# A two-layer hybrid backbone on one core: context rows turned four experts at a time, the last expert's rows added on chip, recurrent products regrouped

## The chip, the cores and the metric

The kernel is one program on one core of a Trainium2 chip. The engines that the rows name are TensorE (PE: products, and transposes that are products with an identity; PEld is its weight load), VectorE (DVE), ScalarE (ACT), GpSimd (POOL) and SyncE (SP, whose queue issues most transfers). The metric is device microseconds of one execution, less is better. The kernel before took 3310.74 us as the median of three runs (3307.70 to 3312.14).

## The reference

Two layers work on 1024 latent tokens of width 1024 beside 256 context tokens. Every layer is a mixer, a residual, and a mixture of 16 experts, and each part is preceded by RMSNorm with a gain, a shift and a scale from a conditioning vector:

```python
# layer 0, chunkwise, both directions (GLA; the SSD half is alike)
att = where(tril, (q*exp(b-b_ref)) @ (k*exp(b_ref-b)).T, 0)        # 64x64 per chunk and head
o   = att @ v + (q*exp(b)) @ S ;  S' = exp(b_last)*S + (k*exp(b_last-b)).T @ v
# layer 1: latent attention, 8 heads of 128, over context and latent keys
o   = softmax(scale*(qn@kn.T + qr@kr.T)) @ v ;  x += m2 * (o @ w_o)
# both layers: each of 16 experts chooses its tokens (cap = 2*T/16)
aff = softmax(h @ w_router) ; g, idx = top_k(aff.T, cap)
hid = silu(h[idx] @ w_gate) * (h[idx] @ w_up)
x[idx] += m5 * g * (hid @ w_down)
```

An expert takes 128 latent rows, and in layer 0 also 32 context rows; layer 1 has no context rows in its mixture. All is float32 outside; the large products run as three products of high and low parts (`mm3`, L135 to L140: high x high L138, high x low L139, low x high L140), and the parts come from `split` (L142 to L145: high part on ScalarE L144, low part on VectorE L145).

## The kernel before

The stages follow each other in time: the recurrent mixer of layer 0 (0 to 883 us), its tail with out-projection, router and choice of tokens (to 1076), the first mixture (to 1887), the latents of layer 1 (to 2010), attention (to 2510), the second tail (to 2681), the second mixture (to 3281), and the end. In the mixers, tails, latents and attention the order of TensorE's work is written out by hand: generators yield an estimate in microseconds of what they have issued, and others are let on by it. In the two mixtures a scheduler orders every engine from the order in which the code issues.

Recurrent mixer. `gla_chain` (L709) works on two heads of ten blocks of 128 tokens, four chains in all. `scores` (L754) makes the masked score tile `am` of a block, on TensorE (L768) and VectorE (L773, L774). The loop at L805 multiplies it with `v` (L820, one product a head) and adds the states' share, up to four 64x64 products a head (L823). For chains 0 and 1 the scores of the next block are issued ahead of a block's products, for chains 2 and 3 behind them; `cov` (L111 and on) holds the side work in microseconds that is issued at each yield.

Tails. `tail` (L1427) runs `mixed` (L1373): tile by tile the out-projection with `wo`, and, one tile late, `router` (L892) and `affinities` (L915). `choose` (L951) searches the thresholds of the 16 experts and leaves `ch_slot` (L1053). In the second tail the eight raw tiles `owr` of `w_o` are loaded by SP (L847) into tiles that share their place with the residual's (tags `rx`, `rxm`, `rh`, `m2`, `m4`, `m3`) and split into two 32 KB tiles `wo`. `router` loads its three row blocks `rg` (L897), transposes them (L899) and folds them into the router's weights.

First mixture. `experts` (L1152), lower half. A `pick` (L1164) makes the row numbers of one expert (`route`, L1069: `rt_hot` by comparison L1073, products L1075, `rt_i` L1079), and GpSimd gathers 128 rows `xg` (L1161); for expert 0 it also runs `top_context` (L1084), which finds the context rows of all experts, and it gathers 32 context rows `xgc`. `prep` turns `xg` (8 transposes of 128x128, L1195) and `xgc` (8 of 32x128, L1203). `gate_up` multiplies per half of the hidden width two chunks of gate and up by `mm3`, and the context rows by the raw chunks in 32 small products (`mm_context`, L1143). `activate` (L1250) makes `sil` for the latent rows and `hc` for the context rows, `turn` (L1262) transposes `sil` (L1266) and `hc` (4 of 32 rows, L1272). `down` (L1276) does four chunks; behind the second and the fourth it multiplies the context rows in 16 small products. `add_rows` (L1296) scales (`ye`, L1297) and scatters with an add (L1298). A raw chunk of 1 MB comes over SP (L1124) into one of eight places (five of a ring and three spare); the low parts of the first two chunks are made by GpSimd in eight pieces (L1132). For the last expert, eight conditioning products (`mod_round`, L296) follow the last product, and then the latents begin: `load` (L1540) reads the first pair of x tiles behind the last scatter, `norm` squares (L1551) and scales (L1555) them, `turn` transposes (L1562). The splits of the latents' weights `wd` precede `norm` in the code.

Second mixture. Only latent rows; `wide_gate_up` (L1217) and `down` of the expert before, as a pipeline: down(e-1) is issued behind gate and up of e, and the turn of e's `sil` (L1266) behind the second and fourth chunk of down(e-1).

## Time and profile before

| what | value |
|---|---|
| median of the runs | 3310.74 us (3307.70 to 3312.14) |
| profiled execution, its own time | 3311.28 us |
| its span, first to last instruction | 3309.5 us |
| mean granted TensorE clock | 0.962 of full speed |
| TensorE busy | 3051.5 us, 92% of the span |
| VectorE, ScalarE, GpSimd busy | 2264.7, 1683.3, 683.7 us |
| moved by DMA | 624.92 MB, mean 189 GB/s |

The page of the profile gives the span in 40 slices of 82.7 us; TensorE's clock, in tenths:

```profile
PEclk8999999999799899999999999999998979999999
```

Busy time is that of instructions on the engine; time that an engine spends waiting is not busy, and the timeline puts it in brackets ahead of the row that ended it, with what released it. A duration of a product in the timeline is longer than its distance to the next one, as products are pipelined: the distance from start to start is what one costs in a dense stretch.

### The profile page before, as it was taken

The numbers are of one execution on the slowest core, as the hardware profiler recorded it, in microseconds if no ns is written. First come the engines' busy times: TensorE is split into PE (matmuls) and PEld (weight loads), VectorE is DVE, ScalarE is ACT, GpSimd is POOL, SyncE is SP. The second block draws the span as 40 slices with busy tenths as digits, with TensorE's granted clock in tenths as the row PEclk, the third lists the DMA queues.
The fourth block names the chain that finished last, engine by engine and source line by source line (L and its number), as shares of the span: only waits on it lengthen the run. The fifth ranks groups of instructions, "written<-read, shape, count | busy, mean of one in ns | idle before, by whom it ended". The sixth has DMA issues, their size and how long they took to land.

```text
span 3309.5 us, 50386 instructions
## 1 busy us (share of the span) xinstructions
PE 3051.5 (92%) x19910; PEld 2382.1 (72%) x19910; DVE 2264.7 (68%) x3526; ACT 1683.3 (51%) x2405; POOL 683.7 (21%) x730
## 2 busy tenths in 40 slices
PE   5999989897897899999999899999998879999997
PEld 4878776686675566666666587888886658887775
DVE  4774463535657777777777676666665588988887
ACT  4444342635221556556566444555553247766675
POOL 3134461426211312212212110000000100111111
PEclk8999999999799899999999999999998979999999
DMA  6112144234764687887887712100106569999995
GB/s 212 47 31 63 41 133 154 57 90 151 243 211 133 235 292 266 286 296 263 286 295 266 253 55 49 30 23 22 26 9 229 188 235 379 373 358 368 367 358 183
DMA packets 252798, 624.92 MB, mean 189 GB/s; under 512 B 47876, under 2 KB 107482, under 8 KB 222866
## 3 DMA queue, kind: packets, MB, share of 16 engines
q1 hardware_dynamic: 227154, 545.17, 45.5%
q0 software_dynamic: 25408, 76.54, 8.3%
q8 instruction: 156, 2.56, 0.3%
q14 instruction: 80, 0.66, 0.1%
HBM read 560.71 MB, written 60.92 MB: 188 GB/s over the span
## 4 chain that ended last, share of the span: by engine, by line
PE 35%; issue 20%; DVE 5%; POOL 4%; ACT 3%; DMA 2%; SPq 0%; POOLq 0%; ACTq 0%; DVEq 0%
PE acc L139 7%; PE acc L140 7%; PE acc L138 7%; PE tp L138 2%; PE tp L139 2%; PE tp L140 2%; PE tp L1788 2%; POOL xl L1298 1%; POOL xc L1298 1%; DMA xl<-ye,rt_i 1%; POOL xg L1161 1%; PE s L1757 1%; PE s L138 1%; PE s L140 1%; PE s L139 1%
## 5 line engine op out<-in xcount | busy, mean ns | idle before, releaser
L145 DVE TENSOR_TENSOR wcl<-wc,wch 128x2048 fp32r<-128x2048 f32 x380 | 874.3, 2308 | 208.0 <-ACT wch L144 206.9
L144 ACT ACTIVATE wch<-wc 128x2048 fp32r<-128x2048 f32 x380 | 728.0, 1918 | 360.5 <-PE acc L140 317.3
L139 PE MATMUL acc<-wcl,xt 128*128 128x512 f32 x1024 | 408.5, 399 | 0.3 <-DVE wcl L145 0.3
L138 PE MATMUL acc<-wch,xt 128*128 128x512 f32 x1024 | 405.9, 404 | 1.8 <-ACT xt L144 1.8
L140 PE MATMUL acc<-wch,xt 128*128 128x512 f32 x1024 | 406.8, 398 | 0.0
L138 PEld LDWEIGHTS acc<-wch,xt 128*128 128x128 f32 x1024 | 194.5, 190 | 72.5 <-issue 25.1
L140 PEld LDWEIGHTS acc<-wch,xt 128*128 128x128 f32 x1024 | 193.9, 189 | 45.4
L139 PEld LDWEIGHTS acc<-wcl,xt 128*128 128x128 f32 x1024 | 194.3, 190 | 43.5 <-DVE wcl L145 0.7
L139 PE MATMUL acc<-wcl,ht 128*128 128x512 f32 x512 | 206.7, 404 | 8.1 <-DVE wcl L145 8.1
L138 PE MATMUL acc<-wch,ht 128*128 128x512 f32 x512 | 209.0, 408 | 0.4 <-ACT wch L144 0.4
L140 PE MATMUL acc<-wch,ht 128*128 128x512 f32 x512 | 202.8, 396 | 0.0
L1298 POOL DMA_INDIRECT xl<-ye,rt_i x31 | 103.1, 3326 | 457.8 <-DVE ye L1297 457.8
L138 PE MATMUL mm<-ahi,w 128*128 128x512 f32 (+1 forms) x480 | 182.6, 380 | 0.0
L139 PE MATMUL mm<-alo,w 128*128 128x512 f32 (+1 forms) x480 | 173.2, 361 | 0.0
L140 PE MATMUL mm<-ahi,w 128*128 128x512 f32 (+1 forms) x480 | 173.1, 361 | 0.0
L1161 POOL DMA_INDIRECT xg<-hl,rt_i x32 | 75.4, 2356 | 400.6 <-issue 176.1
L138 PE MATMUL mm<-w,ahi 128*128 128x256 f32 (+1 forms) x480 | 148.5, 309 | 2.5 <-DVE tm L432 2.5
L144 ACT ACTIVATE pt<-tp 128x512 fp32r<-128x512 f32 (+1 forms) x192 | 98.3, 528 | 101.9 <-PE tp L1788 100.7
L145 DVE TENSOR_TENSOR pt<-tp,pt 128x512 fp32r<-128x512 f32 (+1 forms) x192 | 113.7, 594 | 44.5 <-ACT pt L144 44.3
L140 PE MATMUL mm<-w,alo 128*128 128x256 f32 (+1 forms) x480 | 137.8, 287 | 0.0
L139 PE MATMUL mm<-w,ahi 128*128 128x256 f32 (+1 forms) x480 | 137.7, 287 | 0.0
L138 PE MATMUL acc<-wo,ot 128*128 128x512 f32 x288 | 120.2, 417 | 5.1 <-ACT wo L144 5.1
(530 smaller groups left out, 7090.1 us busy)
## 6 DMA issues: line engine op xcount, KB each, us to landing
wc<-in_w_gate SPq DMA_DIRECT2D x128, 1024.0 KB, 7.4
wc<-in_w_up SPq DMA_DIRECT2D x128, 1024.0 KB, 8.8
wc<-in_w_down SPq DMA_DIRECT2D x128, 1024.0 KB, 8.2
w<-in_w_mod SPq DMA_DIRECT2D x32, 1024.0 KB, 5.3
craw<-in_w_in SPq DMA_DIRECT2D x40, 256.0 KB, 3.1
wm<-in_w_mod SPq DMA_DIRECT2D x8, 1024.0 KB, 10.1
wc<-in_w_mod SPq DMA_DIRECT2D x8, 1024.0 KB, 10.3
xl<-rxm POOLq DMA_DIRECT2D x16, 512.0 KB, 5.5
```

Of the source, the lines that this page charges most:

```text
L138: mm(out, a[0], b[0], start=first, stop=False, skip_group_check=skip)
L139: mm(out, a[0], b[1], start=False, stop=False, skip_group_check=skip)
L140: mm(out, a[1], b[0], start=False, stop=last, skip_group_check=skip)
L144: self.nc.scalar.activation(hi, src, AF.Copy)
L145: self.nc.vector.tensor_sub(lo, src, hi)
L1161: return nc.gpsimd.indirect_dma_start(out=out, out_offset=None, in_=src, in_offset=bass.IndirectOffsetOnAxis(ap=idx, axis=0))
L1298: nc.gpsimd.indirect_dma_start(out=rows[i], out_offset=bass.IndirectOffsetOnAxis(ap=idx, axis=0), in_=y, in_offset=None, compute_op=OP.add)
L1757: nc.tensor.matmul(out, qrl[:, q], krs[:, ks], start=False, stop=True)
L1788: nc.tensor.transpose(p[:, 128 * j:128 * j + 128], pr[:, 128 * (t0 + j):128 * (t0 + j) + 128], self.ident)
```

## The change

Nine edits, in the order of the code:

1. `gla_chain`: in a block first both heads' products with `am`, then the states' products in the order direction, half, head. For chains 0 and 1 the scores of the next block are issued behind the block's products.
2. `router` yields behind its row loads; `mixed` issues the router's weights and the first router's rows at its very start.
3. `mod_round` yields once per chunk of its loop.
4. `affinities` takes a call `amid`; in the first tail's last affinities it makes expert 0's row numbers and issues its gather (`first_rows`).
5. The low parts of the first two chunks of the first mixture go from GpSimd to VectorE, behind the gather.
6. First mixture: context rows of four experts are gathered into one 128-row tile, three experts ahead, and turned by eight full transposes for four experts; `top_context` and the first four gathers are issued between gate and up of the first chunk; both halves of `hc` lie in one 128-row tile and are turned by four full transposes; down's context products of all eight k stand in one group behind the last chunk.
7. Second mixture: the two turns of an expert's `sil` move into the next expert's gate and up (behind chunks 0 and 2).
8. End of the first mixture: the latents' first pair of x tiles is loaded ahead of the last scatter, and the last expert's rows are added to it on chip by products with a 0/1 matrix (`add_last`).
9. Second tail: the eight staging tiles of `w_o` are allocated ahead of `wo`, with the tags in another order, and `wo` consists of 16 tiles of 4 KB a partition.

The core of the diff:

```diff
-    pooled, gated = (2, 0), (0, 2)
+    pooled, gated = (0, 0), (2, 2)
...
-            yield 1.0 / per
+            if k % per == per - 1:
+                yield 1.0
...
+            if not ahead:
+                yield self.cov[4]
+            po = p[:, :, 128:192]
+            for h in range(2):
+                nc.tensor.matmul(po[:, h, :], a[:, h, :], v[:, blk, 64 * h:64 * h + 64], start=True, stop=False,
+                                 skip_group_check=True)
+            ops = [(d, half, h) for d, first in ((0, 0), (1, 3)) for half in range(2) if 2 * blk + half != first
+                   for h in range(2)]
+            for j, (d, half, h) in enumerate(ops):
+                n, ch = 2 * blk + half, slice(64 * h, 64 * h + 64)
+                nc.tensor.matmul(po[64 * half:64 * half + 64, h, :], gates[d][1][ch, 64 * n:64 * n + 64],
+                                 ts[d][ch, n, :], start=False, stop=(j >= len(ops) - 2), skip_group_check=True)
+            nc.scalar.activation(oh[:, blk], po, AF.Copy)
...
-            nc.scalar.activation(oh[:, blk], po, AF.Copy)
+                yield self.cov[4]
...
             nc.sync.dma_start(rows[8 * j:8 * j + 8, :], src.rearrange("(k p) -> k p", p=128))
+        yield None
...
+        if amid:
+            amid()
...
+    def first_rows(self, picked, src, pool):
+
+        nc = self.nc
+        xg = self.ring_chunk(self.ring)[:, :D]
+        fetched = nc.gpsimd.indirect_dma_start(out=xg, out_offset=None, in_=src,
+                                               in_offset=bass.IndirectOffsetOnAxis(ap=picked[0], axis=0))
+        return picked, xg, self.one_behind(fetched, pool)
+
+    def one_behind(self, issue, pool):
+
+        one = pool.tile([128, 1], F32, name="one")
+        with self.tc.issue_after(issue.ins):
+            self.nc.gpsimd.memset(one, 1.0)
+        return one
...
+        def lows(one):
+            for raw, hi, lo in early:
+                nc.vector.scalar_tensor_tensor(lo, raw, one, hi, op0=OP.mult, op1=OP.subtract)
+
...
+            if e == 0 and two:
+                picked[0], xg, one = routes[0][3]
+                lows(one)
+                return xg
+            picked[e] = self.route(e, *routes[0][:2], routes[0][2] if two else pool, tp())
...
+            if early:
+                lows(self.one_behind(fetched, pool))
+            if two and e + 3 < NE:
+                pick_context(e + 3)
+            return xg
+
+        def pick_context(e):
+
+            if e % 4 == 0:
+                four.append(pool.tile([128, D], F32, name="xgc", bufs=1))
+            gather(hs[1], routes[1][0][:, e:e + 1], four[-1][32 * (e % 4):32 * (e % 4) + 32, :])
+
+        def choose_context():
+            routes[1] = self.top_context(routes[1], pool, tp)
+            for c in range(4):
+                pick_context(c)
+
+        def prep_context(xgc):
+            xct = pool.tile([128, KT, 128], F32, name="xct", bufs=1)
+            for half in range(2):
+                p = tp()
+                for j in range(4):
+                    k = 4 * half + j
+                    nc.tensor.transpose(p[:, 128 * j:128 * j + 128], xgc[:, 128 * k:128 * k + 128], self.ident)
+                nc.scalar.activation(xct[:, 4 * half:4 * half + 4, :], p.rearrange("p (k t) -> p k t", t=128), AF.Copy)
+            return xct
...
+                if half == 0 and e % 4 == 0:
+                    turned_rows[0] = prep_context(four.pop(0))
+                xct = turned_rows[0]
...
+                    self.mm_context(cg, xct[:, :, 32 * (e % 4):32 * (e % 4) + 32], [held[2 * (kk // 4) + m][0][:, kk % 4, :] for m in range(2)], kk)
...
+        def both(acc, half=0):
+
+            here, there = slice(64 * half, 64 * half + 64), slice(64 - 64 * half, 128 - 64 * half)
+            sc = pool.tile([128, 512], F32, name="sc", bufs=1)[here]
+            nc.scalar.activation(sc, acc[there, :], AF.Copy)
+            nc.vector.tensor_add(sc, sc, acc[here, :])
...
+            if two:
+                sc = both(cg, half)
+                h = hc[64 * half + 32:64 * half + 64, :]
+                nc.scalar.activation(h, sc[0:32, :], AF.Silu)
+                nc.vector.tensor_mul(h, h, sc[32:64, :])
+            return sil
...
+        def turn_context(hct):
+
+            p = tp()
+            for j in range(4):
+                nc.tensor.transpose(p[:, 128 * j:128 * j + 128], hc[:, 128 * j:128 * j + 128], self.ident)
+            src = p.rearrange("p (k h t) -> p h k t", h=4, t=32)
+            nc.vector.tensor_copy(hct.rearrange("p (h k) t -> p h k t", h=2), src[:, 1::2])
...
-            if two and q % 2:
-                for kk in range(4):
-                    self.mm_context(cy, hct, [held[kk // 2][:, kk % 2, 512 * m:512 * m + 512] for m in range(2)],
-                                    2 * q - 2 + kk)
+            if two and q == 3:
+                with self.tc.issue_after(latest.ins):
+                    for kk in range(KT):
+                        self.mm_context(cy, hct, [held[kk // 2][:, kk % 2, 512 * m:512 * m + 512] for m in range(2)],
+                                        kk)
...
+                        if e and q % 2 == 0:
+                            turn(q // 2, hid[q // 2], late)
...
-                    if e < NE and q % 2:
-                        turn(q // 2, hid[q // 2], ht, None)
+                    if e == NE - 1 and q % 2:
+                        turn(q // 2, hid[q // 2], ht)
...
-            gate_up(e, 0, 0, x, *a0)
+            gate_up(e, 0, 0, x, *a0, choose_context if e == 0 else None)
...
-            turn(1, h1, ht, hct)
+            turn(1, h1, ht)
+            turn_context(hct)
...
+                self.first_x = self.first_tiles(xs[0])
...
+            ye = pool.tile([128, D], F32, name="ye", bufs=1)
+            add_rows(0, idx, gate, ye, ay[0].rearrange("p a f -> p (a f)"))
+            if e == NE - 1:
+                self.add_last(self.first_x, parts, ye.rearrange("p (a f) -> p a f", a=2), pool, psum)
...
+        self.wr = self.router_weights(l, pool)
+        routed = self.router(l, tiles[0][0], pool, psum)
+        next(routed)
...
+                        if n > 1:
+                            routed = self.router(l, late[0], pool, psum)
+                            next(routed)
+                        next(routed)
...
+            if l == 0 and found and not begun:
+                begun.append(self.first_rows(self.route(0, found[0], pay, mc, psum("tp")), self.hd[0], mc))
...
+        begin()
+        routes = [(found[0], pay, mc, *begun)]
...
-        xs = [x_tile() for _ in range(2)]
+        xs = self.first_x
...
-        load(order[0], xs)
...
+
+        xs = [self.first_tile(j) for j in range(2)]
+        for j, x in enumerate(xs):
+            t = 2 * self.order[0] + j - 2
+            self.nc.sync.dma_start(x, src[128 * t:128 * t + 128, :])
+        return xs
+
+    def add_last(self, xs, parts, y, pool, psum):
+
+        nc = self.nc
+        base = 128 * (2 * self.order[0] - 2)
+        tok = pool.tile([128, 256], F32, name="tok_row", tag="xg", bufs=2)
+        nc.gpsimd.iota(tok, pattern=[[1, 256]], base=base, channel_multiplier=0, allow_small_or_imprecise_dtypes=True)
+        at = pool.tile([128, 1], F32, name="tok_at")
+        nc.vector.tensor_add(at, parts[:, 0:1], parts[:, 1:2])
+        hot = pool.tile([128, 256], F32R, name="hot", tag="xg", bufs=2)
+        nc.vector.tensor_scalar(hot, tok, at, None, op0=OP.is_equal)
+        h = [pool.tile([128, 2, 512], F32R, name=f"yh{j}", tag=f"xt{j}", bufs=1) for j in range(2)]
+        self.split(*h, y)
+        for j, x in enumerate(xs):
+            p = psum.tile([128, 2, 512], F32, name="fp", tag="acc", bufs=2)
+            for m in range(2):
+                for i in range(2):
+                    nc.tensor.matmul(p[:, m], hot[:, 128 * j:128 * j + 128], h[i][:, m], start=(i == 0), stop=(i == 1))
+            nc.vector.tensor_add(x, x, p.rearrange("p a f -> p (a f)"))
...
-                    wo = [pool.tile([128, KT, D], F32R, name=f"wo{j}") for j in range(2)]
+                    tags = ("m2", "m4", "m3", "rh", "rx", "rx", "rxm", "rxm")
+                    staged = [pool.tile([128, D], F32, name="owr", tag=t, bufs=2 if "x" in t else 1) for t in tags]
+                    wo = [Rows([pool.tile([128, D], F32R, name=f"wo{j}{k}") for k in range(KT)]) for j in range(2)]
...
-                    tags = ("rx", "rxm", "rx", "rxm", "rh", "m2", "m4", "m3")
-                    stage = lambda k: pool.tile([128, D], F32, name="owr", tag=tags[k], bufs=1 if k > 3 else 2)
```

## Rows read from the trace of the kernel before

**Rows 1.** Table by stretch, two steady ones: busy time by engine, PEclk, DMA share, GB/s.
```profile
1150.00:1200.00 50.00, 50.00 (x288) 33.08 (x286) 37.84 (x32) 29.64 (x25) 10.73 (x5) 1.00 0.83 284
2750.00:2900.00 150.00, 150.00 (x695) 122.06 (x694) 136.06 (x97) 107.56 (x76) 17.44 (x9) 1.00 0.97 378
```
**Rows 2.** Waits of the queue of SP, first mixture: total us, times, longest.
```profile
SPq L1124 <- PE cg L1143: 651.6, 120, 13.4
```
**Rows 3.** Timeline of TensorE, an expert change of the first mixture: start, duration, instruction.
```profile
1227.82 0.40 PE L138 MATMUL acc<-wch,ht 128*128 128x512 f32 x1
1228.14 0.68 PE L1203 MATMUL tp<-ident,xgc 32*128 32x32 f32 x8
...
1229.09 0.40 PE L140 MATMUL acc<-wch,ht 128*128 128x512 f32 x1
...
1230.03 0.60 PE L1266 MATMUL tp<-ident,sil 128*128 128x128 f32 x4
1230.56 0.43 PE L1272 MATMUL tp<-ident,hc 32*128 32x32 f32 x4
1230.92 0.50 PE L138 MATMUL acc<-wch,ht 128*128 128x512 f32 x1
...
1235.74 0.51 PE L138 MATMUL acc<-wch,ht 128*128 128x512 f32 x1
1236.09 0.39 PE L139 MATMUL acc<-wcl,ht 128*128 128x512 f32 x1
1236.32 0.39 PE L140 MATMUL acc<-wch,ht 128*128 128x512 f32 x1
```
**Rows 4.** The tile `ye`, second mixture, two stretches: min/median/max ns, first and last start.
```profile
L1297 DVE SCALAR_TENSOR_TENSOR ye<-acc,rt_g,m x5: 1277/1278/1280, 2750.0 to 2894.9; 128x1024 f32<-128x1024 f32 x5
...
L1297 DVE SCALAR_TENSOR_TENSOR ye<-acc,rt_g,m x8: 1283/1284/1285, 2967.7 to 3230.8; 128x1024 f32<-128x1024 f32 x8
```
**Rows 5.** Timeline of TensorE at the first mixture's start; idle before and releaser in brackets.
```profile
1082.05 0.20 PE L1100 MATMUL tp<-ident,tf 16*32 16x16 f32 x1 [5.84 <-ACT tf L1097]
1087.57 1.09 PE L1195 MATMUL tp<-ident,xg 128*128 128x128 f32 x4 [5.31 <-DMA xg<-hl,rt_i]
```
**Rows 6.** Timeline of GpSimd there.
```profile
1077.15 1.71 POOL L1161 DMA_INDIRECT xg<-hl,rt_i  x1 [4.40 <-DMA wdr<-in_w_dkv]
```
**Rows 7.** Timeline of VectorE there.
```profile
1071.08 0.29 DVE L1053 TENSOR_TENSOR ch_slot<-ch_both 128x128 bf16<-128x128 f32 x1
...
1074.82 0.67 DVE L1073 TENSOR_TENSOR rt_hot<-slots,ch_slot 128x1024 bf16<-128x1024 bf16 x1
```
**Rows 8.** Timeline of TensorE between the first mixture and the latents.
```profile
1883.24 3.64 PE L296 MATMUL mod<-wc,sT 128*32 128x256 f32 x64
1901.56 1.47 PE L1562 MATMUL tp<-ident,x 128*128 128x128 f32 x4 [14.69 <-DVE x L1555]
```
**Rows 9.** Timeline of ScalarE there.
```profile
1895.90 1.06 ACT L1551 ACTIVATE junk<-x 128x1024 bf16<-128x1024 f32 x1 [6.38 <-DMA x<-xl]
```
**Rows 10.** Timeline of TensorE at the second tail's start.
```profile
2515.13 0.79 PE L138 MATMUL acc<-wo,ot 128*128 128x512 f32 x1 [5.12 <-ACT wo L144]
...
2538.47 0.27 PE L899 MATMUL rl<-ident,rg 24*128 24x24 f32 x1 [6.51 <-DMA rg<-in_norm_ffn]
```
**Rows 11.** Timeline of the queue of SP there.
```profile
2510.15 4.32 SPq L847 DMA_DIRECT2D owr<-in_w_o  x8
```
**Rows 12.** Timeline of TensorE, a late expert change of the second mixture.
```profile
2996.68 0.50 PE L139 MATMUL acc<-wcl,ht 128*128 128x512 f32 x1 [0.87 <-DVE wcl L145]
```
**Rows 13.** Timeline of VectorE there.
```profile
2994.34 2.29 DVE L145 TENSOR_TENSOR wcl<-wc,wch 128x2048 fp32r<-128x2048 f32 x1
```
**Rows 14.** Timeline of TensorE, one block of a recurrent chain.
```profile
560.23 0.33 PE L820 MATMUL sA<-v,am 128*128 128x64 f32 x2
...
561.63 0.39 PE L138 MATMUL mm<-ahi,w 128*128 128x256 f32 x1
```
**Rows 15.** Waits of TensorE from 500 to 883 us.
```profile
PE sA L820 <- DVE am L774: 5.9, 8, 1.1
```

133 lines of the change are left out of this document (43 added, 90 removed).

## The prediction

> **What bounds the kernel now.** The views were read in this order. The table by stage comes first: TensorE is at work 3051.5 us of the 3309.5 us span, and a steady stretch of either mixture stage shows it busy in every microsecond of the window [rows 1]. So in the steady stretches only fewer or cheaper TensorE instructions count, or waits that come later. Second, the waits of the queue that loads the first mixture's weights: 651.6 us over 120 waits, and what they wait for is `cg`, TensorE's own last read of the chunk; the loads are paced by TensorE and not TensorE by them, at a DMA share of 0.83 [rows 1, 2]. Third, TensorE's timeline at the joints of stages, where the idle time before a row and its releaser stand in brackets: 5.84 + 5.31 us ahead of the first mixture [rows 5], 14.69 us ahead of the latents [rows 8], 5.12 + 6.51 us in the second tail [rows 10]. Last, TensorE and VectorE at an expert change of the second mixture [rows 12, 13] and the recurrent products [rows 14, 15].
>
> **The change part by part.** The sum is made against the profiled execution: 3311.28 us, of which 3309.5 is the span and 1.8 lies around it; the median of the runs is 3310.74, 0.5 us lower. "Step" is the start-to-start distance of one 128x512 product in a steady stretch, 0.23 us (1236.09 to 1236.32 in [rows 3]).
>
> *First mixture, steady* (16 experts, TensorE full, so every microsecond of instructions is worth one). (a) The eight 32-row context transposes: from the product before them at 1227.82 to the product but one behind, 1229.09, are 1.27 us; two steps would be 0.46, so 0.81 go [rows 3]. In their place eight full transposes stand once for four experts. Four full ones (`sil`) take 1230.03 to 1230.56, 0.53 us, so eight are 1.06, with entry and exit some 1.2, a quarter of it 0.3: net -0.5. (b) `hc`: two groups of four small transposes at 0.36 (1230.56 to 1230.92) become one of four full ones at 0.53: -0.19 [rows 3]. (c) Down's context products: two groups become one. The first product behind such a group takes 0.35 to the next instead of 0.23 (1235.74 to 1236.09), and the last one ahead of small products 0.32 (1227.82 to 1228.14) [rows 3]; one entry and exit fewer saves 0.21, and some 0.1 at the joint between the halves is an estimate; I take 0.3. Together -1.0 an expert, times 16 is **-16** (ends -10, if every transpose switch costs what the dearest shows, and -19). What must not be late: half 1 of `hc` is read right behind `sil` of half 1 as before, and the evictions on ScalarE and VectorE become fewer. The context gathers go three experts ahead, so none is waited for in the steady part.
>
> *First mixture, start.* The gather of expert 0's rows is issued at 1077.15, and its rows end the wait at 1087.57, 10.4 us later [rows 5, 6]. It hangs on `rt_hot`, which VectorE takes at 1074.82, though its input was ready at 1071.08 + 0.29 = 1071.37 [rows 7]. Inside the last affinities it can start there: 3.4 us earlier. The low parts move from GpSimd to VectorE behind the gather; VectorE has idle time in the wait. And `top_context`, for which TensorE stands still 5.84 us [rows 5], moves between gate and up of the first chunk, where products cover it. Its four gathers of 32 rows come before the second chunk's context products. Take 3.4 and half of the 5.3 to 5.8 us that the two waits then share: **-6** (ends -3: the same wait for the rows, only earlier; -10: both).
>
> *End of the first mixture.* Before, x is loaded behind the last scatter; the first square starts at 1895.90 when the load lands, the first transpose at 1901.56 after 14.69 us of idle TensorE [rows 8, 9]. Now x is in place. The chain is `ye`, its two splits and eight one-hot products (8 x 0.23, twice that at half clock, so 2 to 4) behind the modulation products that end at 1883.24 + 3.64 = 1886.9 [rows 8], two adds of 1.28 as long as `ye` [rows 4], square, scale, transposes. From 1886.9 + 2 to 4 + 1.3 the first square is due at 1890 to 1892 instead of 1895.90. Against it: the splits of `wd` lie on ScalarE and VectorE at the same time and are passed or waited for. **-6** (ends -3, -9).
>
> *Second tail.* The eight raw `w_o` loads are all issued at 2510.15, once attention's last product has read the tiles they overlay; TensorE stands 5.12 us, until 2515.13 [rows 10, 11]. The staging moves to tiles whose last readers come earlier in attention, so that loads and the first splits can come ahead of 2510, and the 5.12 go. The page's slice from 2482 to 2565 has a granted clock of 0.8 of full speed: a product at half clock costs a second step, and I estimate ten of them at each of the two restarts, 10 x 0.23 = 2.3, of which one set goes surely. The router's row loads are issued behind residual loads, and TensorE waits 6.51 us for them, until 2538.47 [rows 10]; issued at the very start they are there. 5.1 + 6.5 + 2.3 = **-14** (ends -8: choose and the residual chain stay as they are and swallow part; -18).
>
> *Second mixture.* Expert periods: (2894.9 - 2750.0) / 4 = 36.2 us early, (3230.8 - 2967.7) / 7 = 37.6 late [rows 4]. In the late ones TensorE waits 0.87 us at the transposes of `sil` for `wcl` [rows 12], while VectorE has both halves of `sil`, the next `xt`, `wcl` (from 2994.34, 2.29 us) [rows 13], `ht` and the next `wcl` one behind the other. The change moves both halves of this turn into the next expert's gate and up: the burst is stretched over some 10 us more. If the late period falls to the early one, 9 x 1.4 = -12. I take **-9** (ends 0 and -12).
>
> *Recurrent products.* 40 blocks; one costs TensorE 1.40 us (560.23 to 561.63) [rows 14]. Regrouped so that row halves alternate, I estimate 1.1 to 1.2: 40 x -0.2 to -0.3 is -8 to -12. Against it: for chains 0 and 1 the scores come behind the products, so `am` has 2.8 us of side work to hide in (the two entries of the code's own cover list, 1.6 + 1.2), instead of a whole block. In the rows `am` is waited for 5.9 us in 8 waits [rows 15]. 20 blocks at about 0.5 more: +10 at worst. I take **-4** (ends +5 and -12).
>
> Other parts (`mod_round` yielding per chunk, router weights first, GpSimd's `one`) issue the same instructions beside full engines: 0, and +-1 each. Sum: -16 - 6 - 6 - 14 - 9 - 4 = -55, 3311.3 - 55 = 3256; the run's median is 0.5 lower, and I leave 1 us for joints: 3257.
>
> **The Trainium skill.** The second mixture moved 378 GB/s over 150 us at the 36.2 us period [rows 1], and the waits there are for VectorE. The Trainium skill, "DMA: Bandwidth & Descriptors", Specifications, gives one core about 358 GB/s from HBM. By that rule the early period's 378 x 36.2 = 13.7 MB an expert would want 38.2 us, no gain is possible in that stage, and the sum is -46, 3265. The trace disagrees with the rule (378 measured over four experts); I keep it as a rival, as loads may yet limit later experts.
> For the recurrent products, "TensorE: Matmul & The Clock Gate", Part 3, says that a weight load overlaps products in flight only where its row group differs. By it the alternation hides a load that now is open, and the estimate of 1.1 would be an upper end; the trace of before shows only the old order.
>
> **The rivals.**
> 1. *Transfers take over the second mixture.* For: DMA share 0.97 [rows 1]. Against: weights are waited for by the split's buffers, TensorE by the split and not by a load [rows 12]. Term 0 instead of -9: 3265.
> 2. *Half-gains at the joints.* SP issues in order, so the early `w_o` loads can stand behind something that waits for attention; the router rows alone then gain (-6.5), and the start and latents chains each move by -3: -55 + 7.5 + 3 + 3 = -41, with the second mixture's term gone too -32: 3270 to 3279.
> 3. *Slower: down's raw chunks.* The context products now wait for the last chunk, so the first two raw chunks are held 24 products and a group longer: 24 x 0.23 + 2.5 = 8 us per expert. The loads are issued the moment a buffer is free (mean wait 651.6 / 120 = 5.4 us [rows 2]), so the next chunk lands up to 8 us later, and landing takes 8.2 us by the page's table of issues. If their slack is under 8 - 3.5 us, TensorE stalls more than 55 / 16 = 3.5 us an expert and the whole is lost; with no slack at all 16 x 8 - 55 = +73, 3384; at 4.5 us of stall, +17, 3328. Against: TensorE has no wait for weights in the window, and half of all chunks stay in separate buffers.
> 4. *The change does not do what it says:* the new staging tiles lie on others that attention still reads. Then the tail gains 6.5 of 14: 3264.
>
> **How the numbers follow.** The forecast with its own range 3240 to 3268 (which takes in rivals 1 and 4): 0.74. Rival 2: 0.15. No net change, gains offset by partial rival 3: 0.04. Rival 3 past its point: 0.07. A range of 3237 to 3284 leaves under 0.2 out. What this measurement tells from no change is about 0.2%, 6.6 us: faster 0.90, same 0.04, slower 0.06.
>
> **What would show it.** After: the distance of `ye` in the first mixture 1.0 us an expert shorter (right), or longer with weights named ahead of TensorE (rival 3); the first `xg` transposes within 4 us of 1083; no idle over 9 us ahead of the latents; `wo` products right behind attention, no half clock, no wait for `rg`; late periods of the second mixture near 36.2 (else rival 1); recurrent blocks at or under 1.2 us with `am` waits under 15 us in all. Wrong would be: TensorE idle for weights in either mixture, or a time above 3284.

## The result and the profile after

The changed kernel took 3267.23 us (median of 4 runs, 3266.88 to 3270.06), the kernel before 3309.22 us on the same chip (4 runs, 3306.80 to 3312.14): ratio 0.9872, interval 0.9857 to 0.9887, 42 us faster. The forecast was 3257 us with a range of 3237 to 3284: direction right, size 10 us too good. The profiled execution took 3267.22 us (span 3265.4), 44.1 us less than that of before.

The page of after; slices are now 81.6 us, `PEclk` is the granted clock in tenths:

```profile
PE 2999.9 (92%) x19758; PEld 2365.1 (72%) x19758; DVE 2272.8 (70%) x3517; ACT 1682.3 (52%) x2398; POOL 660.9 (20%) x725
PEclk8999989998898899999999999999999989999999
```

TensorE's busy time fell by 51.6 us, more than the span. Cut at marks that both traces have (first `wo` product of a tail, first `xt` product, `ye` of an expert, first `wd` product), the two spans differ like this:

| stretch | before, us | after, us | difference | forecast |
|---|---|---|---|---|
| start to first `wo` product of tail 0 | 887.0 | 874.2 | -12.8 | -4 |
| tail 0, to first `xt` product | 202.3 | 200.6 | -1.7 | -6 with the next |
| first product to `ye` of expert 0 | 55.0 | 59.3 | +4.4 | |
| 14 experts, first mixture | 691.6 | 670.6 | -21.0 | -14 |
| `ye` of expert 15 to first `wd` product | 25.8 | 24.6 | -1.2 | -6 |
| latents and attention | | | 0 | 0 |
| attention's last product to first `wo` | 5.4 | 2.7 | -2.7 | -14 with the next |
| first to last `wo` product | 121.5 | 116.3 | -5.2 | |
| on to `ye` of expert 0 | 113.4 | 111.7 | -1.6 | |
| 14 experts, second mixture | 516.9 | 516.7 | -0.2 | -9 |
| end | 42.6 | 41.0 | -1.5 | |

The last expert of the first mixture (45.7 and 45.4 us) stands in no row; that of the second lies in the end. Of the first row, 2.6 us is no part of the change: from 170 to 200 us, ahead of the recurrent chains, the granted clock was 0.89 in the execution of before and 1.00 in that of after, and an experiment with the changed kernel's code in this stretch has 0.89 there again. Stretches of equal code differ by up to 5.5 us between the executions here. Tail 0 is the worst: 200.6 us in after, 200.1 to 205.6 in the nine experiments that leave it as it is. So the -1.7 of tail 0 shows nothing by itself, the medians of experiments move by some us for reasons that are not their edits, and verdicts below are read by stretch.

**Recurrent products** (answers [rows 14, 15]): TensorE's timeline inside the block of [rows 14] before, then one block after, then its waits from 500 to 875 us (total us, times, longest).

```profile
560.49 0.45 PE L823 MATMUL sA<-ts,b 64*64 64x64 f32 x8
560.88 0.43 PE L820 MATMUL sA<-v,am 128*128 128x64 f32 x2
```

```profile
555.61 0.55 PE L823 MATMUL sA<-v,am 128*128 128x64 f32 x4
556.09 0.46 PE L829 MATMUL sA<-ts,b 64*64 64x64 f32 x16
556.48 0.70 PE L780 MATMUL sA<-b,k 64*32 64x64 f32 x40
```

```profile
PE sA L823 <- DVE am L786: 17.2, 11, 5.9
```

A block is 555.61 to 556.48, 0.87 us instead of 1.40; behind it stand the next scores. The sixteen states' products in one group take 0.39 us (556.09 to 556.48), no more than each group of eight did (560.49 to 560.88). The 20 blocks of chains 0 and 1 look like this one; those of chains 2 and 3 are mixed with one another. Over all 40 blocks the groups of these products, waits inside them included, take 44.2 us from start to start instead of 60.2: 0.40 us a block. The stage kept 10.2 of these 16 us. The waits for `am` rose from 5.9 to 17.2 us.

**First mixture, start** (answers [rows 5 to 7]): timeline of VectorE, the queue of SP, GpSimd and TensorE, in order of time.

```profile
1059.22 0.28 DVE L1066 TENSOR_TENSOR ch_slot<-ch_both 128x128 bf16<-128x128 f32 x1
...
1059.67 0.44 SPq L1593 DMA_DIRECT2D wdr<-in_w_dkv  x1
1060.15 0.43 SPq L1152 DMA_DIRECT2D wc<-in_w_gate  x1
...
1062.43 1.39 POOL L1101 DMA_INDIRECT wc<-hl,rt_i  x1 [2.25 <-DVE rmx L949]
...
1070.31 1.97 PE L1244 MATMUL tp<-ident,wc 128*128 128x128 f32 x8 [6.03 <-DMA wc<-hl,rt_i]
1074.77 0.80 PE L149 MATMUL acc<-wch,xt 128*128 128x512 f32 x1 [2.48 <-ACT wch L1156]
1077.30 0.80 PE L150 MATMUL acc<-wcl,xt 128*128 128x512 f32 x1 [1.74 <-DVE wcl L1194]
1085.82 0.80 PE L150 MATMUL acc<-wcl,xt 128*128 128x512 f32 x1 [2.55 <-DVE wcl L1194]
```

The chain did get shorter: from `ch_slot` to the issue of the gather 3.2 us (before 6.1), from there to the end of the wait for rows 7.9 (before 10.4). Only the first of the two is steady: in the nine experiments that leave this stage as it is, the second took 8.2 to 10.1 us. Then TensorE waits for weights, which it did not before: 2.48 us for `wch`, ahead of expert 0's first product, and inside its 59.3 us 1.74 and 2.55 for `wcl`. The queue of SP shows where the loads are. The first weight chunk is issued at 1060.15, behind 20 raw loads `wdr` for the latents; in the trace of before five chunks had been issued between 913.29 and 954.30. In after `first_rows` takes its rows' tile from the weights' own ring ahead of those loads, and they come behind it.

**First mixture, steady** (answers [rows 2, 3]): TensorE's timeline at an expert change, its groups in nine experts (busy us, mean ns, idle before), SP's waits.

```profile
1217.87 0.61 PE L1319 MATMUL tp<-ident,hc 128*128 128x128 f32 x4
1218.24 0.48 PE L149 MATMUL acc<-wch,ht 128*128 128x512 f32 x1
...
1222.58 0.50 PE L151 MATMUL acc<-wch,ht 128*128 128x512 f32 x1 [0.32 <-DVE ht L156]
```

```profile
L1319 PE MATMUL tp<-ident,hc 128*128 128x128 f32 x36 | 5.5, 277 | 0.0
L1228 PE MATMUL tp<-ident,xgc 128*128 128x128 f32 x16 | 2.1, 272 | 0.0
```

```profile
SPq L1152 <- PE cg L1171: 612.0, 118, 14.5
```

`xgc` is 16 transposes in nine experts (before 72), `hc` 36 (before 72); a group of four full `hc` takes 0.37 us (1217.87 to 1218.24), no more than each of the two small groups that it replaces (0.36 [rows 3]). The queue waits for TensorE as before, and TensorE for no weight. It does wait, once in every expert, for the low part of `ht` that VectorE makes: 2.8 us in nine experts, none in before.

**End of the first mixture** (answers [rows 8, 9]): timeline of ScalarE, VectorE, TensorE.

```profile
1855.92 5.55 ACT L155 ACTIVATE wd<-wdr 128x704 fp32r<-128x704 f32 x8 [1.58 <-DVE yce L1345]
...
1858.23 2.35 DVE L1728 TENSOR_TENSOR xf<-xf,fp 128x1024 f32<-128x1024 f32 x2 [0.35 <-PE fp L1727]
1860.50 6.50 DVE L156 TENSOR_TENSOR wd<-wdr,wd 128x704 fp32r<-128x704 f32 x8
1866.92 0.16 DVE L162 TENSOR_SCALAR rs_v<-ss 128x2 f32<-128x2 f32 x1
...
1868.74 0.48 PE L1630 MATMUL tp<-ident,xf 128*128 128x128 f32 x1 [9.61 <-DVE xf L1623]
```

x is there and the idle time fell from 14.69 to 9.61 us, but the one-hot products now stand ahead of it. The sums end at 1860.58; then VectorE does eight splits of `wd`, 6.50 us, before the norm's `rs_v`.

**Second tail** (answers [rows 10, 11]): timeline of SP, TensorE, ScalarE.

```profile
2469.69 4.31 SPq L857 DMA_DIRECT2D owr<-in_w_o  x8
...
2479.67 0.51 PE L149 MATMUL acc<-wo,ot 128*128 128x512 f32 x1 [2.41 <-ACT wo L155]
2481.12 0.79 PE L150 MATMUL acc<-wo,ot 128*128 128x512 f32 x1 [0.95 <-DVE wo L156]
...
2516.70 1.06 ACT L892 ACTIVATE rh<-rxm 128x1024 f32<-128x1024 f32 x1 [6.49 <-DMA hl<-rh]
...
2521.53 0.40 PE L945 MATMUL rl<-fold,rht 128*128 128x16 f32 x2 [1.98 <-DVE rht L944]
```

The loads start 7.3 us ahead of attention's last product and not behind it, and the wait of 6.51 us for `rg` is gone. At 2499 us the tail had gained 44.8 - 32.8 = 12.0 us since attention's end; 4 us of that came back. The last rows give a reading of how, which no run tested: `rh` is one buffer, and ScalarE stands 6.49 us for the store of the tile before, issued beside the second mixture's weight loads (370 GB/s from 2500 to 2522); TensorE waits 1.98 us for `rht`, and a granted clock of 0.73 follows from 2522 to 2528. Behind the first restart it was 0.81 (2482 to 2488).

**Second mixture** (answers [rows 1, 4, 12, 13]): the tile `ye` early and late; the table by stretch; VectorE and TensorE late; TensorE's waits from 2700 us on.

```profile
L1345 DVE SCALAR_TENSOR_TENSOR ye<-acc,rt_g,m x5: 1278/1279/1279, 2707.7 to 2852.6; 128x1024 f32<-128x1024 f32 x5
L1345 DVE SCALAR_TENSOR_TENSOR ye<-acc,rt_g,m x8: 1283/1284/1286, 2925.8 to 3188.3; 128x1024 f32<-128x1024 f32 x8
```

```profile
2718.00:2863.00 145.00, 145.00 (x674) 117.94 (x674) 131.24 (x93) 104.34 (x73) 23.04 (x8) 1.00 0.97 376
2927.00:3190.00 263.00, 256.43 (x1172) 206.22 (x1171) 229.53 (x159) 180.59 (x127) 39.11 (x15) 1.00 0.96 364
```

```profile
2952.22 0.16 DVE L1090 COPY rt_s<-tp 128x5 f32<-128x5 f32 x1 [0.15 <-PE tp L1088]
2952.47 2.29 DVE L156 TENSOR_TENSOR wcl<-wc,wch 128x2048 fp32r<-128x2048 f32 x1
...
2954.81 0.50 PE L150 MATMUL acc<-wcl,ht 128*128 128x512 f32 x1 [0.87 <-DVE wcl L156]
```

```profile
PE acc L150 <- DVE wcl L156: 8.4, 11, 0.9
```

Early periods are (2852.6 - 2707.7) / 4 = 36.2 us, late ones (3188.3 - 2925.8) / 7 = 37.5: as before. In the late experts the scheduler still puts all eight `sil` transposes in one place, 27.1 us behind `ye` (27.0 before), and the wait of 0.87 us stands where it stood. In the early experts the turns did move, to 4.1 and 15.8 us behind `ye`, and their period did not change. The loads are not the limit: in the late experts they land 25 us or more ahead of their split, in both kernels.

### The profile page after: what moved, and what is told of

It reads as the page before. It is cut to its first block, busy times and chain, and to the rows that moved or that the text cites. A ratio compares the mean times of both kernels' runs of the same rounds, so it can differ in the third digit from the quotient of the medians.

```text
span 3265.4 us, 49999 instructions
## 1 busy us (share of the span) xinstructions
PE 2999.9 (92%) x19758; PEld 2365.1 (72%) x19758; DVE 2272.8 (70%) x3517; ACT 1682.3 (52%) x2398; POOL 660.9 (20%) x725
## 4 chain that ended last, share of the span: by engine, by line
PE 55%; DVE 6%; ACT 4%; issue 2%; DMA 1%; POOL 0%; ACTq 0%; POOLq 0%; DVEq 0%; SPq 0%
PE acc L151 11%; PE acc L150 11%; PE acc L149 11%; PE cg L1171 5%; PE tp L149 2%; PE tp L150 2%; PE tp L151 2%; DVE wcl L156 2%; PE tp L1885 2%; ACT wch L155 2%; PE tp L1244 1%; PE s L1854 1%; PE s L149 1%; PE s L151 1%; PE s L1853 1%
## 5 line engine op out<-in xcount | busy, mean ns | idle before, releaser
L156 DVE TENSOR_TENSOR pt<-tp,pt 128x512 fp32r<-128x512 f32 (+1 forms) x192 | 113.7, 594 | 44.8 <-ACT pt L155 44.6
```

Source lines behind the costliest of these rows:

```text
L156: self.nc.vector.tensor_sub(lo, src, hi)
```

## The experiments

Ratios are to the kernel before. Diffs are against the changed kernel and cut to their core.

**Recurrent products.** Theory: the regrouping gave the stage its 10 us, and the scores' new place is its cost (the longer waits for `am`).

```diff
             for h in range(2):
-                nc.tensor.matmul(po[:, h, :], a[:, h, :], v[:, blk, 64 * h:64 * h + 64], start=True, stop=False,
...
-            for j, (d, half, h) in enumerate(ops):
...
+                nc.tensor.matmul(po[:, h, :], a[:, h, :], v[:, blk, ch], start=True, stop=not ops,
...
+                for j, (out, l, r_) in enumerate(ops):
+                    nc.tensor.matmul(out, l, r_, start=False, stop=(j == len(ops) - 1), skip_group_check=True)
```

(the whole loop over the blocks as before, scores ahead; the next run keeps the new products and moves only the scores)

```diff
-            if not ahead:
-                yield self.cov[4]
+            if ahead and blk + 1 < NT:
+                nxt = scores(blk + 1)
+            yield self.cov[4]
...
-            if ahead and blk + 1 < NT:
-                nxt = scores(blk + 1)
-                yield self.cov[4]
```

> Kernel after with the loop over the blocks of a recurrent chain put back as before (products head by head, scores of chains 0 and 1 ahead). Theory A (the 12 us that the recurrent mixer became shorter by come from the regrouped products, 1.39 to 0.87 us a block, less 9 us of new waits for the score tile): the first out-projection product moves back from 874.2 to about 884 to 886 us, blocks cost 1.39 again, waits for the score tile fall to about 6 us, the time is 3277 to 3279. Rival B (the mixer is shorter because conditioning products are let on per chunk, or by the clock): the mixer stays within 3 us of the kernel after, time 3265 to 3270.

> Kernel after with the regrouped products, but the scores of the next block issued ahead of a block's products for chains 0 and 1, as before. Theory A (the moved scores cost waits: 17 us against 6): the waits for the score tile fall to under 8 us, the blocks stay near 0.9 to 1.0 us, the mixer ends 3 to 8 us earlier, time 3259 to 3264. Rival B (the waits only show time that the chain loses elsewhere anyway; the place of the scores is paid back by cheaper changes between products and scores): mixer within 2 us of the kernel after, 3265 to 3269.

The old loop: 3279.51 us (3274.08 to 3280.20), ratio 0.9899 [0.9879, 0.9918]. From the chains' first turn of `k` to the first `wo` product it took 423.8 us, after 412.2, before 422.4. New products with the scores ahead: 3269.87 (3266.09 to 3272.82), 0.9871 [0.9852, 0.9891], stretch 414.3. The waits for `am`, first of the old loop, then of the second kernel:

```profile
PE sA L832 <- DVE am L786: 7.8, 9, 1.7
```

```profile
PE sA L824 <- DVE am L786: 10.5, 10, 1.8
```

Equal code takes 411.5 to 413.1 us in this stretch. With the scores ahead in both kernels, the old products cost 423.8 - 414.3 = 9.5 us more; that is the regrouping. `mod_round` yields per chunk in both, so it is not the cause. The scores' place is not a cost: ahead of the products the `am` waits fall by 6.7 us and the stage is 2 us longer, not shorter. So these waits were not what the stage's length hung on; what it did hang on was not followed.

**Second mixture.** Theory: the late period stays because the scheduler leaves the turns in one place; pinned one group later, they let the period fall. Rival: it is the loads.

```diff
-                            turn(q // 2, hid[q // 2], late)
+                            with self.tc.issue_after(latest.ins):
+                                turn(q // 2, hid[q // 2], late)
```

(`latest`: the last product of the gate/up chunk just issued)

> Kernel after with the two turns of an expert's hidden rows in the second mixture pinned behind the chunk of the next expert's gate and up behind which the code issues them. Theory A (in the late experts the scheduler issued these turns early, all eight in one place between the down products, so the change did not take effect there; the wait of 0.87 us for the low part at that place makes the late period 37.5): late periods fall to 36.2 to 36.4, time 3256 to 3260. Rival B (transfers set the late period, 36.2 would need more than they give): the wait moves to the weights and the period stays at 37 to 37.6, time 3265 to 3268.

3286.59 us (3284.72 to 3288.40), 0.9927 [0.9908, 0.9945]: 19 us slower than after, 16.5 of it in the 14 experts of the second mixture. First the `ye` rows of its late experts, then its waits:

```profile
L1346 DVE SCALAR_TENSOR_TENSOR ye<-acc,rt_g,m x8: 1283/1284/1286, 2928.9 to 3205.6; 128x1024 f32<-128x1024 f32 x8
```

```profile
PE acc L150 <- DVE wcl L156: 17.0, 18, 1.8
```

Late periods of 39.5 us, more waits for `wcl`, and loads that land some 30 us ahead of their split. Theory and rival fell alike. Next theory: down's first low parts are split too late, behind `silu`; splitting two chunks ahead of it gives the 1.3 us back. The second kernel has the pinned turns as well.

```diff
+                    if e:
+                        ahead.extend(wide_chunk(e - 1, q, wd) for q in range(2))
+                    with self.tc.issue_after(self.hi_split.ins):
+                        hid = [activate(a[half], None) for half in range(2)]
-                    hid = [activate(a[half], None) for half in range(2)]
...
-                _, hi, lo = wide_chunk(e, q, wd)
+                _, hi, lo = ahead.pop(0) if ahead else wide_chunk(e, q, wd)
```

> Kernel after; in the second mixture the first two down chunks of the expert before are split ahead of an expert's silu on ScalarE (in the early experts the trace has this order, in the late ones only one chunk is split ahead and ScalarE stands 3.0 us before silu). The turns stay where the scheduler puts them. Theory A (the late period of 37.5 comes from the low part of the second down chunk, which VectorE makes behind silu and xt): late periods 36.2 to 36.6, the 0.87 us waits for wcl gone, time 3257 to 3261. Theory B (the eight turns in one place are what delays the low parts): wait stays, period 37 to 37.6, 3265 to 3269. Theory C (transfers bound the late experts): period stays and the wait moves to ScalarE's split waiting for a load.

> Kernel e5 with the turns pinned into the next expert's gate and up as in e3. Theory A and B: the late experts now have the order of the early ones on all engines, period 36.2 to 36.3 throughout, time 3256 to 3259 (e3 lost because a pinned turn with only one chunk split ahead leaves TensorE waiting 1.7 us and then running at half clock for some products). Theory C (transfers): period stays over 37 and loads land less than 5 us ahead of their split.

3277.24 us (3274.25 to 3280.89), 0.9908 [0.9891, 0.9924], and 3280.81 (3278.40 to 3283.41), 0.9915 [0.9898, 0.9931]: slower than after, both. By stretch the 14 experts take 518.4 and 527.1 us (after 516.7), so the first gains and loses almost nothing here: its theory A fell, with late periods of 35.3 to 41.1 us, and TensorE also waits 3.9 us for gathered rows. VectorE and TensorE of the second kernel at a late change:

```profile
3038.47 0.16 DVE L1090 COPY rt_s<-tp 128x5 f32<-128x5 f32 x1 [2.78 <-PE tp L1088]
3038.55 2.29 DVE L1163 TENSOR_TENSOR wcl<-wc,wch 128x2048 fp32r<-128x2048 f32 x1
...
3040.90 0.50 PE L150 MATMUL acc<-wcl,ht 128*128 128x512 f32 x1 [1.67 <-DVE wcl L1163]
```

The first row is the cause in small. VectorE takes its work in order, and stands 2.78 us at `rt_s`, the copy of the next expert's routes, because TensorE issues the route's products behind 22 `ht` products (12 in the early experts of every version, 10 in the late ones of after); the split that TensorE needs next is queued behind that copy. So: pin the second down chunk's products behind the route's.

```diff
+                        with self.tc.issue_after(self.routed.ins) if q == 1 and e + 2 < NE else nullcontext():
+                            down(e - 1, q, late, None, ay, None)
-                        down(e - 1, q, late, None, ay, None)
```

> Kernel e6, and the products of the second down chunk pinned behind the route's products (rt_hot). In e6's late experts TensorE does the route's products only after 22 products of down instead of 12, VectorE stands 2.8 us at the copy rt_s that waits for them, and the next low part is queued behind it. Theory A (the late period is set by what stands ahead of the low parts in VectorE's queue, not by transfers): late periods fall to 36.2 to 36.6 in every late expert, time 3256 to 3260. Rival B (weights or something else that only late experts have): periods stay over 37, 3265 or more.

3263.21 us (3261.91 to 3263.47), 0.9849 [0.9830, 0.9869]. Late `ye` rows, then the waits, then the table:

```profile
L1347 DVE SCALAR_TENSOR_TENSOR ye<-acc,rt_g,m x8: 1282/1284/1284, 2927.5 to 3184.3; 128x1024 f32<-128x1024 f32 x8
```

```profile
PE acc L150 <- DVE wcl L1163: 2.9, 9, 0.5
```

```profile
2927.00:3184.00 257.00, 254.92 (x1170) 205.47 (x1170) 228.02 (x157) 181.76 (x126) 38.96 (x14) 1.00 0.98 372
```

A late period of 256.8 / 7 = 36.7 us and 14 experts in 509.1 us (527.1 without the last pin, 516.7 in after). Between the last two kernels the order of VectorE's queue was the wait: VectorE stands 0.45 us at `rt_s` now. Theory A is right in the cause and short in the amount: six late periods are 36.8 us, over its 36.6, and the time is over its 3260; by medians the interval overlaps with that of after. In after itself the copy waits 0.15 us only, and the late low part stands behind `sil` and `xt`; that the split ahead of `silu` removes this is seen only together with both pins. The loads give 372 GB/s when asked.

**Start of the first mixture.** Theory: the prefetch that `first_rows` lost. Four chunk loads are put ahead of it again.

```diff
             if l == 0 and found and not begun:
+                for j in range(4):
+                    w = (self.io["w_gate"], self.io["w_up"])[j % 2][0]
+                    raw = self.ring.tile([128, 4, 512], F32, name="wc", tag="wc", bufs=self.nraw)
+                    self.nc.sync.dma_start(raw, w[0, 512 * (j // 2):512 * (j // 2) + 512, 0:512]
+                                           .rearrange("(k p) f -> p k f", p=128))
+                    self.pre.append(raw)
```

> Kernel after; the loads of the first four weight chunks of the first mixture are issued in the code ahead of the gather of expert 0's rows (same places in the ring). In before, five chunks were loaded between 913 and 955 us; in after the first is issued at 1060 us, behind 20 loads for the latents, at a DMA share of 1.05. Theory A (the rows come 15 to 17 us earlier but expert 0 now waits for its weights: 59.3 us from its first product to ye instead of 55.0): loads are back before 960, the first product comes 1.5 to 3 us earlier, expert 0 takes 53 to 56 us, time 3258 to 3264. Rival B (expert 0 is slow because the search for the context rows stands between gate and up, and VectorE makes the low parts late): expert 0 stays over 58 us, time 3265 to 3268.

3264.96 us (3261.34 to 3267.41), 0.9866 [0.9849, 0.9883]. TensorE's timeline at the first products:

```profile
1073.69 1.97 PE L1248 MATMUL tp<-ident,wc 128*128 128x128 f32 x8 [7.82 <-DMA wc<-hl,rt_i]
1075.49 0.80 PE L150 MATMUL acc<-wch,xt 128*128 128x512 f32 x1
```

The products follow the transposes at once, and the waits of 2.48, 1.74 and 2.55 us are gone. Expert 0 takes 54.6 us instead of 59.3; the next one gives 1.7 back, so 3 us are left. By medians, whose intervals overlap, it is 2 us; by the stretch it is shown, and rival B falls.

**Ahead of the latents.** Theory: the norm waits behind the eight `wd` splits; rival: VectorE's work is one sum in either order.

```diff
+        norm(xs)
         for k in range(KT):
             self.split(wd[0][:, k, :], wd[1][:, k, :], self.wd_raw[k])
-        norm(xs)
```

> Kernel after with the squares and the scaling of the latents' first pair issued ahead of the splits of the latents' weights. Theory A (the gain at the start of the latents was lost because the 6.5 us of weight splits on VectorE, 1860.5 to 1867, stand between the sums and the scaling): the first transpose of the pair comes 2.5 to 4 us earlier (idle of TensorE before it 9.6 to about 6), and the first latent product 1 to 4 us earlier, as splits now run beside the transposes; time 3263 to 3266. Rival B (the splits only move behind, and the first latent product waits for them): first latent product within 0.5 us of the kernel after, 3266 to 3268.

3267.54 us (3263.44 to 3269.80), 0.9870 [0.9852, 0.9888]. VectorE and TensorE:

```profile
1864.06 5.70 DVE L156 TENSOR_TENSOR wd<-wdr,wd 128x704 fp32r<-128x704 f32 x7
...
1863.54 0.48 PE L1630 MATMUL tp<-ident,xf 128*128 128x128 f32 x1 [5.09 <-DVE xf L1623]
1870.27 2.04 PE L1630 MATMUL tp<-ident,xf 128*128 128x128 f32 x6 [2.50 <-DVE af L1636]
```

The idle time ahead of the first transpose falls by 4.5 us, and `ye` to the first `wd` product is only 0.4 us shorter (24.3): seven splits now hold `af`. The rival is right; it is the amount.

**Staging of the second tail.** Old staging tiles, all else as changed.

```diff
-                    tags = ("m2", "m4", "m3", "rh", "rx", "rx", "rxm", "rxm")
-                    staged = [pool.tile([128, D], F32, name="owr", tag=t, bufs=2 if "x" in t else 1) for t in tags]
...
+                    tags = ("rx", "rxm", "rx", "rxm", "rh", "m2", "m4", "m3")
+                    stage = lambda k: pool.tile([128, D], F32, name="owr", tag=tags[k], bufs=1 if k > 3 else 2)
```

> Kernel after with the staging tiles of w_o and the two 32 KB tiles as in before; the early router rows stay. Theory A (staging is worth the 2.7 us of idle that went ahead of the first product and some clock; the router rows are worth the 6.5 us wait): attention's last product to the first w_o product 5.4 us again instead of 2.7, no wait for rg, last w_o product 2 to 5 us later against attention's end, time 3268 to 3272. Rival B (the later chain of residual, norm and affinities takes it back): last w_o product within 1 us of the kernel after, 3266 to 3268.

3274.04 us (3271.59 to 3277.76), 0.9894 [0.9877, 0.9912]. SP and TensorE:

```profile
2482.90 4.04 SPq L857 DMA_DIRECT2D owr<-in_w_o  x8
...
2488.05 0.80 PE L149 MATMUL acc<-wo,ot 128*128 128x512 f32 x1 [5.21 <-ACT wo L155]
```

The loads are again issued behind attention's last product and the idle time is back: staging is worth 5.5 - 2.7 = 2.8 us. The rest of the 7 us between the medians lies ahead of attention, in equal code. First to last `wo` product stays at 116.4, so the 5.2 us there are not the staging's; that they come from the early router rows is read from the wait for `rg` that is gone, and no run took these rows back.

**Down's context products** in two groups again, so that two raw chunks are let go earlier (rival 3 undone).

```diff
-            if two and q == 3:
+            if two and q % 2:
                 with self.tc.issue_after(latest.ins):
-                    for kk in range(KT):
+                    for kk in range(4):
...
-                                        kk)
+                                        2 * q - 2 + kk)
```

> Kernel after with down's context products in two groups again (behind the second and the fourth chunk, both pinned there). Theory A (the single group saves an entry and an exit, and holding the raw chunks costs nothing): the mean distance of ye in the first mixture, 47.90 us in the kernel after, becomes 48.1 to 48.3, time 3270 to 3273. Rival B (holding four raw chunks until the end delays loads and costs 0.3 us or more an expert): distance the same or shorter, 3262 to 3267.

3265.80 us (3262.16 to 3271.95), 0.9861 [0.9837, 0.9885]. The tile `ye` of 15 experts, its first and last start:

```profile
L1345 DVE SCALAR_TENSOR_TENSOR ye<-acc,rt_g,m x15: 1277/1278/1279, 1140.0 to 1808.3; 128x1024 f32<-128x1024 f32 x15
```

(1808.3 - 1140.0) / 14 = 47.74 us against 47.90 (equal code: 47.87 to 47.90): one group instead of two gains nothing and costs about 0.16 us an expert, and theory A fell. TensorE's timeline of this run has the group back behind the second chunk:

```profile
1225.90 1.92 PE L1171 MATMUL cg<-wc,hct 128*32 128x512 f32 x16
```

Start to start in nine experts, two groups cost TensorE 2.8 us more in the context products and their neighbours, 0.32 an expert, which is the 0.3 that theory A prices. But in these 1.92 us VectorE makes the low part of `ht`: this run has no wait for it, and the route's products with the wait behind them take 4.65 us instead of 8.79, 0.46 an expert. The difference is the 0.14 to 0.16. Rival B has the number and not the cause: no weight is waited for in either kernel. The last expert and the start of the latents are shorter too, by 0.6 and 1.7 us, which was not followed.

**Two mends together:** the pinned route with the early loads.

> Kernel e9 and the preloaded chunks of e7 together: if both act in their own stage, the gains add: e7's 2 to 5 us at expert 0 of the first mixture and, under theory A of e9, about 9 to 10 us in the second mixture: 3251 to 3257. If e9's theory falls: 3262 to 3266.

3256.22 us (3252.82 to 3261.01), 0.9826 [0.9806, 0.9846]: 14 experts of the second mixture in 509.1 us, expert 0 of the first in 54.6. The gains add, and this version, which keeps the single group of context products, beats both kernels: its interval lies under that of the changed one (0.9857 to 0.9887).

## Why the prediction came out so

**First mixture, steady: -1.0 an expert forecast, -1.5 measured.** Right for the transposes, too small in the sum, and step (c) failed. Start to start, in nine experts: context transposes 5.50 to 1.58 us, `hc` 6.52 to 3.35, `sil` 9.52 to 7.09, gate/up products 206.47 to 201.87, `ht` products 106.64 to 104.21, down's context products 33.38 to 32.13. `sil`, gate/up and `ht` add up to 1.05 us an expert, and the forecast had priced only the edited groups and their own entry and exit. About 0.4 of it is no entry at all: a gate/up product inside a dense row steps 0.228 us instead of 0.233, and no run shows why. In step (c) the price was right, 0.32 for the 0.3 taken; what failed is the list of what must not be late, which did not have `ht` on it. The group that moved had covered the making of its low part, and without it the route's products with the wait behind them cost 0.46 us an expert more. Rival 3 had the sign of that, by another cause and far under its 3.5.

**Recurrent products: -4 forecast, about -10.** What failed is the size of the regrouping, 0.2 to 0.3 us a block, an estimate that no row carried, for a measured 0.40 on average (0.53 in the blocks of chains 0 and 1; the forecast took one such block for all 40). The +10 bound for `am` failed too: its waits rose to 17.2 us, over the 15 that the forecast named as its sign, and putting the scores back did not shorten the stage. The Trainium skill, "TensorE: Matmul & The Clock Gate", Part 3, on weight loads that overlap only in another row group, agrees in direction with the 0.39 us for sixteen products in alternating row halves as for eight in one half; order and grouping change together in every run here, so none shows that this rule is the reason.

**Start of the first mixture: -6 forecast, +2.7 with tail 0 counted in.** The chain from `ch_slot` to the end of the wait for rows gained 5.4 us (16.5 to 11.1), of which 2.9 or more stand in the nine experiments too; so the 3.4 us of the forecast nearly held, and the half of the 5.3 to 5.8 us only in part. What failed is that nothing else was taken to be late next: the forecast followed the gather and not the queue of SP, on which the weight loads moved from 913 to 1060 us. TensorE idle for weights is what the forecast itself named as a sign of being wrong. The run with early loads took 4.7 us off expert 0, of which the next gave 1.7 back.

**End of the first mixture: -6 forecast, -1.2.** The text said that the splits of `wd` "are passed or waited for"; they are waited for, 6.50 us on VectorE. The run with the norm first shows that the order does not mend it. The idle time ahead of the latents, 9.61 us, is over the 9 that the forecast named as its sign.

**Second tail: -14 forecast, -7.9 by the `wo` marks.** The wait of 5.12 us became 2.41 + 0.95, as ScalarE splits the first rows only at 2478; the `rg` wait went and the half clock did not: the granted clock is 0.81 from 2482 to 2488 and 0.73 from 2522 to 2528. There the products stand 0.43 us apart, and 0.23 at full clock. So the 2.3 us taken for it did not come as forecast; the slice read as 0.8 is 0.90 by the table of that stretch. The -7.9 is close to the lower end of 8, and to the half-gain that rival 2 named for this joint, though not by its way: the loads stood behind nothing.

**Second mixture: -9 forecast, -0.2.** This is the largest miss. The cause of the wait was read rightly (VectorE's queue), the effect of the edit was not: in the early experts the turns moved and the period stayed 36.2, in the late ones the scheduler did not place them where the code's order puts them, and put there by hand they make it worse. Rival 1 gave the right number for a wrong reason: the loads land 25 us or more ahead of their split. The 358 GB/s of the Trainium skill, "DMA: Bandwidth & Descriptors", Specifications, did not bind here: 376 GB/s early, and 372 late once the order was mended, with a period 0.8 us shorter. The Trainium skill, "DMA: Bandwidth & Descriptors", Bandwidth, gives this figure for two cores of one HBM domain that load at once; this program runs on one core.

**The sum.** Start, latents, second tail and second mixture fell short by 8.7 + 4.8 + 6.1 + 8.8 = 28 us. The recurrent stage (6), the steady mixture (7), the clock ahead of the chains (2.6) and the two small rows at the table's end (3) gave 19 of it back. That the total was near is in part luck.

**To carry to other kernels.** When an in-order engine is named as the releaser, look at what stands at the head of its queue and who must issue that, before moving work around it. When a step takes a tile from a ring that other loads share, follow those loads too. And price a removed group of small instructions with its neighbours' entries, not alone, and ask what another engine was doing while it ran.

**Not expected of the hardware.** Sixteen 64x64 products whose row halves alternate take TensorE 0.39 us in one group, as eight in one row half did. And two groups of context products are cheaper for the kernel than one of twice the length (47.74 and 47.90 us an expert), though dearer for TensorE by 0.32 us: the first of them covers a wait.
